# Seven places for the split weights of the upper output projection, a first half of norm 2 without GpSimd, and six FFN weight pieces split ahead

## The chip, the cores and the metric

The kernel runs on one core of one Trainium2 chip. A core has TensorE for matmuls (PE in the profile, with its weight loads as PEld), VectorE (DVE), ScalarE (ACT), GpSimd (POOL) and SyncE (SP), which here issues most DMA transfers between the chip's memory and the core's two on-chip memories, SBUF and PSUM. Each engine works through its own list of instructions in order; where one needs what another makes, it waits on a semaphore, and everything behind it in its list waits with it. The metric is the device time of one execution in microseconds (us). Three runs of the kernel before gave 3312.47, 3306.03 and 3312.3 us; their median is 3312.3 us.

## The reference, cut to what matters

One layer of a hybrid backbone is applied to 128 context tokens and 512 latent tokens, 640 tokens in all, with width D = 2048 and an FFN of width 5632. The mixers (a two-directional RWKV-7 scan and a chunked gMLP) give `[o_a, o_b]`. The change lies behind them:

```
x = x + g1 * (jnp.concatenate([o_a, o_b], axis=-1) @ lp['w_out'])
h = _rmsnorm(x, lp['norm2_g']) * (1.0 + sc2) + sh2
ff = (jax.nn.silu(h @ lp['w_ffn_gate']) * (h @ lp['w_ffn_up'])) @ lp['w_ffn_down']
return x + g2 * ff, s_fin
```

`_rmsnorm` divides each token by the root of the mean square over its 2048 channels. A final norm follows. Everything is computed in float32.

## The kernel before

Activations lie transposed, channels on the 128 partitions and tokens along the free axis: `x1T[kb]` is block kb of 16 channel blocks, 128 x 640. The 640 tokens are two halves of 320, `t1` (hf 0) and `t2` (hf 1).

A float32 product is made out of three matmuls of the type fp32r. Each operand is split into a rounded part `hi` and a rest `lo`, and for each 128 x 128 block of weights the sum of hi·hi, hi·lo and lo·hi is kept. A weight piece is 512 rows by 128 columns (256 KB), which is four blocks. `split` loads it with one DMA of SyncE into `raw` (L165), ScalarE casts it to `hi` (L166), and VectorE subtracts to get `lo` (L167). The tiles come from the pool `st` with three places each: three raw, three hi, three lo. For an FFN piece `load_plain` (L1382) and `parts` (L1391, L1392) do the same, and take their hi and lo from the same `st`.

**The upper half of the output projection.** The product with `w_out` runs in two steps; the change touches the second, over the rows of the mixer outputs whose hi and lo are `oh` and `ol`. `four_blocks(hf, m, q)` makes one piece and its 12 matmuls (L1447, L1448, L1449) for output block m, token half hf and quarter q. For hf 0 and then hf 1, for m from 0 to 15, two pieces are multiplied, so that there are 64 pieces and 768 matmuls; of hf 0 the first AHEAD = 6 pieces with q = 0 are done ahead of that loop. After each block `add_out` (VectorE, L1026) adds the result to `x1T[m]`, a DMA stores it (L1466), and `squares` squares it (ScalarE, L1412) and adds it up over a group of mostly four blocks (GpSimd, L1418). `stats` turns a group's sum into a matmul with a matrix of ones (TensorE, `ss`, L1428); after the last group of a half it makes the factor `rs` of the norm (L1431 VectorE, L1432 ScalarE, L1433 VectorE). Before, `stats` is called one block after the block that closed a group.

**Norm 2, half t1.** During hf 1, at each odd m, `first_half(m // 2)` normalizes two channel blocks of t1: GpSimd multiplies by `rs` (L1364), and VectorE multiplies and adds the modulation (L1365). For the first eight blocks `operand` also makes the FFN operand `xo`: a cast on ScalarE (L1354) and a subtraction on VectorE (L1355). GpSimd's list holds these multiplications among the sums of squares L1418 that TensorE's `ss` waits for.

**The start of the FFN.** The first two of the 44 FFN blocks (f 0 and 1 of the planner's order) are done plainly. `plain(e)` (L1534 to L1536) multiplies four pieces (gate and up weights, two channel ranges) with the operands; `first_blocks` calls plain(0) to plain(6) and does the rest of norm 2 between them: `second_half` (L1487 VectorE, L1489 ScalarE), `sums` (L1497 to L1502, VectorE), further `operand`s, `plain_out` (the gate's result, L1543 and L1544) and at the end `stores(0)`, which makes sums of the two results on GpSimd (L1703 to L1710) and stores them. Behind it the other 42 blocks run in pairs of seven products (`seven`, L1602 to L1604): GpSimd makes the combinations of weights (L1515). Their weights are loaded by `load_w` (L1688) into the pool `gu`, which has RAWB = 13 places for raw pieces and opens when the pools of the projection are closed. The loads are pulled one by one from an iterator as pieces are consumed.

A scheduler of the language sets the final place of an instruction in each engine's list, so that the order of the code is not always the order of the list.

## Time and profile before

| | us |
|---|---|
| median of three runs | 3312.3 |
| lowest and highest run | 3306.03, 3312.47 |
| profiled execution | 3317.92 |
| its span in the profile | 3316.1 |
| TensorE busy | 3151.8 (95% of the span) |
| VectorE busy | 2409.3 (73%) |
| ScalarE busy | 1452.3 (44%) |
| GpSimd busy | 1278.7 (39%) |

The profile shows one execution. Its span is the time between the first and the last recorded instruction; the execution's own time is 1.8 us more, and 5.6 us above the median of the runs. The mean clock granted to TensorE was 0.98 of full speed. TensorE is busy almost all the time; a microsecond in which it waits in the middle of the kernel, or in which its clock is lowered, is a microsecond of the kernel's time unless a later wait would have taken it anyway. The projection's second step and the start of the FFN lie from about 1462 to 1675 us of the span.

### The profile page before, as it was taken

Reading aid. Unit: us, or ns where it says so; the run is one execution under the profiler, and the core shown is the slowest. Engines: PE = TensorE matmul, PEld = TensorE weight load, DVE = VectorE, ACT = ScalarE, POOL = GpSimd, SP = SyncE. Lnnn points to the kernel's source line nnn. Section 1 sums busy time; section 2 is a strip of 40 time slices with the busy share of each in tenths; the row PEclk is TensorE's granted clock in tenths of the full one; section 3 lists DMA queues with packets and bytes.
Section 4 is the critical chain, followed back from the end, with each engine's and each line's share of the span. In section 5 each row is a group of like instructions: output and inputs, shape, how many; then the busy total and the mean of one; then the engine's idle time right before and its main releaser. Section 6 shows DMA issues by size and latency. Waiting matters only on the chain.

```text
span 3316.1 us, 72388 instructions
## 1 busy us (share of the span) xinstructions
PE 3151.8 (95%) x28216; PEld 2912.2 (88%) x28216; DVE 2409.3 (73%) x4152; ACT 1452.3 (44%) x3163; POOL 1278.7 (39%) x1114
## 2 busy tenths in 40 slices
PE   6899999999999999998999999999999999999996
PEld 3688788778877888888999999999999999999996
DVE  4448767766866677767877777877778787877787
ACT  3334444444443444334644444444444445444365
POOL 0001122222212113333155655656656555555543
PEclk8899999999999999999999999999999999999998
DMA  8767676767667488735534343443443454553453
GB/s 318 247 180 212 184 203 186 184 182 202 187 179 217 129 273 272 237 118 158 166 103 123 118 121 118 120 128 108 125 127 103 129 185 150 162 156 116 139 162 118
DMA packets 740142, 550.88 MB, mean 166 GB/s; under 512 B 140712, under 2 KB 673208, under 8 KB 730968
## 3 DMA queue, kind: packets, MB, share of 16 engines
q1 hardware_dynamic: 727480, 532.57, 53.7%
q0 software_dynamic: 9984, 13.13, 1.7%
q8 instruction: 222, 3.64, 0.5%
q14 instruction: 120, 0.98, 0.1%
q10 hardware_dynamic: 2336, 0.57, 0.1%
HBM read 437.79 MB, written 110.95 MB: 165 GB/s over the span
## 4 chain that ended last, share of the span: by engine, by line
PE 74%; DVE 10%; DMA 6%; issue 5%; POOL 3%; ACT 2%; SPq 0%; DVEq 0%; ACTq 0%; POOLq 0%
PE P L1604 15%; PE P L1603 15%; PE P L1602 15%; PE big L188 4%; PE big L190 4%; PE big L189 4%; PE pG L636 2%; PE pm L881 2%; DMA raw<-in_w_in_dram 2%; DMA wt<-in_w_mod_dram 1%; PE big L1013 1%; DVE lo L1392 1%; PE big L1449 1%; PE big L1447 1%; PE big L1448 1%
## 5 line engine op out<-in xcount | busy, mean ns | idle before, releaser
L1602 PE MATMUL P<-xo,hi 128*128 128x320 f32 x2352 | 728.2, 310 | 3.3 <-ACT hi L1391 3.3
L1604 PE MATMUL P<-xo,lo 128*128 128x320 f32 x2352 | 728.3, 310 | 2.0 <-DVE lo L1392 1.9
L1603 PE MATMUL P<-xo,hi 128*128 128x320 f32 x2352 | 728.1, 310 | 0.0
L1392 DVE TENSOR_TENSOR lo<-raw,hi 128x512 fp32r<-128x512 f32 x532 | 513.7, 969 | 169.1 <-ACT hi L1391 164.5
L1391 ACT CAST hi<-raw 128x512 fp32r<-128x512 f32 x532 | 330.7, 622 | 496.8 <-PE P L1603 389.7
L188 PE MATMUL big<-h_hi,hi 128*128 128x320 f32 x1376 | 452.3, 329 | 8.4 <-ACT hi L166 4.9
L1602 PEld LDWEIGHTS P<-xo,hi 128*128 128x128 f32 x2352 | 442.7, 188 | 3.5 <-ACT hi L1391 3.5
L1604 PEld LDWEIGHTS P<-xo,lo 128*128 128x128 f32 x2352 | 442.6, 188 | 2.8 <-DVE lo L1392 2.8
L1603 PEld LDWEIGHTS P<-xo,hi 128*128 128x128 f32 x2352 | 442.6, 188 | 0.0
L190 PE MATMUL big<-h_hi,lo 128*128 128x320 f32 x1376 | 435.1, 317 | 1.3 <-DVE lo L167 1.3
L189 PE MATMUL big<-h_lo,hi 128*128 128x320 f32 x1376 | 435.0, 316 | 0.7 <-DVE h_lo L345 0.7
L1515 POOL TENSOR_TENSOR raw<-raw 128x512 f32<-128x512 f32 x252 | 407.7, 1627 | 14.9 <-DVE lo L1392 3.3
L1604 PE MATMUL P<-xd,lo 128*128 128x320 f32 x1232 | 383.5, 311 | 14.0 <-DVE lo L1392 13.9
L1602 PE MATMUL P<-xd,hi 128*128 128x320 f32 x1232 | 382.0, 310 | 2.7 <-ACT hi L1391 0.9
L1603 PE MATMUL P<-xd,hi 128*128 128x320 f32 x1232 | 380.6, 309 | 0.0
L167 DVE TENSOR_TENSOR lo<-raw,hi 128x512 fp32r<-128x512 f32 x268 | 187.2, 701 | 218.9 <-ACT hi L166 214.8
L188 PEld LDWEIGHTS big<-h_hi,hi 128*128 128x128 f32 x1376 | 263.7, 192 | 75.7 <-issue 48.3
L166 ACT CAST hi<-raw 128x512 fp32r<-128x512 f32 x268 | 165.9, 619 | 274.7 <-PE big L189 124.4
L1391 ACT CAST hi<-rawd 128x512 fp32r<-128x512 f32 (+1 forms) x288 | 168.9, 587 | 241.5 <-PE P L1603 196.3
L189 PEld LDWEIGHTS big<-h_lo,hi 128*128 128x128 f32 x1376 | 264.3, 192 | 7.0 <-issue 3.5
L190 PEld LDWEIGHTS big<-h_hi,lo 128*128 128x128 f32 x1376 | 263.7, 192 | 7.5 <-DVE lo L167 3.0
L1604 PEld LDWEIGHTS P<-xd,lo 128*128 128x128 f32 x1232 | 231.2, 188 | 20.4 <-DVE lo L1392 19.9
(378 smaller groups left out, 6270.0 us busy)
## 6 DMA issues: line engine op xcount, KB each, us to landing
wt<-in_w_mod_dram SPq DMA_DIRECT2D x96, 1024.0 KB
raw<-in_w_ffn_gate_dram SPq DMA_DIRECT2D x182, 256.0 KB
raw<-in_w_ffn_up_dram SPq DMA_DIRECT2D x182, 256.0 KB
rec<-d_S SPq DMA_DIRECT2D x80, 576.0 KB
raw<-in_w_in_dram SPq DMA_DIRECT2D x172, 256.0 KB
rawd<-in_w_ffn_down_dram SPq DMA_DIRECT2D x128, 256.0 KB
raw<-in_w_out_dram SPq DMA_DIRECT2D x96, 256.0 KB
xd<-d_os SPq DMA_DIRECT2D x66, 320.0 KB
```

The source lines that it names most:

```text
L166: S.copy(hi, raw)
L167: V.tensor_sub(lo, raw, hi.bitcast(F32))
L188: TE.matmul(halves[hf], hi[:, k, :], h_hi[:, kb, s], start=(kb == 0), stop=False)
L189: TE.matmul(halves[hf], hi[:, k, :], h_lo[:, kb, s], start=False, stop=False)
L190: TE.matmul(halves[hf], lo[:, k, :], h_hi[:, kb, s], start=False, stop=(kb == KB - 1))
L636: TE.matmul(two[h][:, cc - c0, :], XZ[:, cc, h, :, :].rearrange("p s t -> p (s t)"), R[:, cc, :, :].rearrange("p s t -> p (s t)"), start=T ...
L1391: S.copy(hi[:, 0:nk], raw[:, 0:nk])
L1392: V.tensor_sub(lo[:, 0:nk], raw[:, 0:nk], hi[:, 0:nk].bitcast(F32))
L1515: G.tensor_tensor(out=o[:, 0:nk], in0=p[:, 0:nk], in1=q[:, 0:nk], op=ALU.subtract)
L1602: TE.matmul(ps, hi[:, k, :], xk[:, 0, :], start=f, stop=False)
L1603: TE.matmul(ps, hi[:, k, :], xk[:, 1, :], start=False, stop=False)
L1604: TE.matmul(ps, lo[:, k, :], xk[:, 0, :], start=False, stop=l)
```

## The change

Five things are changed.

1. All upper `w_out` pieces but the first six take their raw tile from a pool `wraw` with four places and hi and lo from a pool `wo` with seven places, in place of three and three.
2. `first_half` handles one channel block: VectorE multiplies by `rs`, and ScalarE applies scale and bias of the modulation in one activation. GpSimd has no part in it. It runs at m = 2 to 13 with one block each and at m = 14 and 15 with two each; the eight operand pairs are made at m = 4 to 11.
3. `stats` runs later: the oldest group is taken when m % 4 is 1, or when the group ends at block 12 or beyond.
4. Six FFN pieces are loaded into a pool `wfirst` of their own at m = 6, 7 and 8 of hf 1, and split into hi and lo tiles of the pool `pre` when the loop is over. Two more are loaded at m = 15 into `st` and split as before. These eight pieces are the whole of plain(0) and plain(1).
5. plain(0) and plain(1) run before the projection's pools are closed and without pulling loads; only then does `gu` open and do the first loads into it begin. `stores(0)` moves from the end of `first_blocks` to a hook of the first block of the seven-product stage (f = 2, third product).

```diff
-    def split(src, nk):
+    def split(src, nk, praw=None, pool=None):
         n = 512 // nk
-        raw = st.tile([P, nk, n], F32, tag="raw", name="raw", bufs=3)
-        hi = st.tile([P, nk, n], F32R, tag="hi", name="hi")
-        lo = st.tile([P, nk, n], F32R, tag="lo", name="lo")
+        praw, pool = praw or st, pool or st
+        raw, hi, lo = (p.tile([P, nk, n], t, tag=k, name=k) for p, t, k in
+                       ((praw, F32, "raw"), (pool, F32R, "hi"), (pool, F32R, "lo")))
...
-    def first_half(j):
-        for kb in (j, j + 8):
-            x = x1T[kb]
-            G.tensor_tensor(out=x[:, t1], in0=x[:, t1], in1=rs[:, t1], op=ALU.mult)
-            V.tensor_scalar(x[:, t1], x[:, t1], modc[4][:, kb, 0:1], modc[3][:, kb, 0:1], op0=ALU.mult, op1=ALU.add)
-        if j < 4:
-            operand(1, j, x1T[j][:, t1])
-            operand(2, j, x1T[j + 8][:, t1])
+    HALVES = [j + 8 * i for j in range(8) for i in range(2)]
+    def first_half(kb):
+        x = x1T[kb][:, t1]
+        V.tensor_tensor(out=x, in0=x, in1=rs[:, t1], op=ALU.mult)
+        S.activation(x, x, AF.Identity, scale=modc[4][:, kb, 0:1], bias=modc[3][:, kb, 0:1])
...
+    NPRE = 6
...
+                if i < NPRE:
+                    raw = wfirst.tile([P, 4, P], F32, tag="raw", name="raw")
+                    nc.sync.dma_start(raw, src)
+                    held_w.append(raw)
...
+    np_, wraw, pre, wo, wfirst = (phn.enter_context(tc.tile_pool(name=n, bufs=b)) for n, b in
+                          (("np", 2), ("wraw", 4), ("pre", 1), ("wo", 7), ("wfirst", NPRE)))
...
-            hf, m, sq = sqs.pop()
+            hf, m, sq = sqs.pop(0)
...
-            hi, lo = split(w_out[0, 4 * q * P:(4 * q + 4) * P, m * P:(m + 1) * P], 4)
+            hi, lo = split(w_out[0, 4 * q * P:(4 * q + 4) * P, m * P:(m + 1) * P], 4,
+                           *((wraw, wo) if q or hf or m >= AHEAD else ()))
...
-                if hf and m == KB - 1:
-                    for _ in range(3):
+                if hf and m in (6, 7, 8, KB - 1):
+                    for _ in range(2):
                         next(first)
-                if sqs:
+                if sqs and (sqs[0][1] >= 12 or m % 4 == 1):
                     stats()
...
-                if hf and m % 2:
-                    first_half(m // 2)
+                if hf and m > 1:
+                    for kb in HALVES[m - 2:m - 1] if m < 14 else HALVES[2 * m - 16:2 * m - 14]:
+                        first_half(kb)
+                    if 4 <= m < 12:
+                        j, i = divmod(m - 4, 2)
+                        operand(1 + i, j, x1T[j + 8 * i][:, t1])
+        for i, raw in enumerate(held_w):
+            hi, lo = (pre.tile([P, 4, P], F32R, tag=f"{t}{i}", name=t) for t in ("hi", "lo"))
+            S.copy(hi, raw)
+            V.tensor_sub(lo, raw, hi.bitcast(F32))
+            READY.append((hi, lo))
...
     def first_blocks():
-        plain(0)
-        plain(1)
...
-        stores(0)
...
+    loads = iter(())
+    plain(0)
+    plain(1)
+    phn.close()
+    cbx.close()
+    gux = ExitStack()
+    gu = gux.enter_context(tc.tile_pool(name="gu", bufs=2))
...
     loads = itertools.chain(first, load_w(2), load_w(3))
...
+            if f == 2 and o == 2:
+                stores(0)
```

Three places show how the lists of the engines change. In the rows that follow, a name's number tells one tile of a name from another. The first place is GpSimd's list where hf 1 of the projection begins. `sumq` are sums of squares, `sq2` a block's squares, `x1T` a block of the residual stream, and `rs2` the norm's factor. Before:

```order
L1418 TENSOR_TENSOR sumq_19345<-sumq_19302,sq2_19343 128x320
L1418 TENSOR_TENSOR sumq_19388<-sumq_19345,sq2_19386 128x320
L1364 TENSOR_TENSOR x1T_13554<-x1T_13554,rs2_18691 128x320
L1364 TENSOR_TENSOR x1T_13546<-x1T_13546,rs2_18691 128x320
L1364 TENSOR_TENSOR x1T_13553<-x1T_13553,rs2_18691 128x320
L1364 TENSOR_TENSOR x1T_13545<-x1T_13545,rs2_18691 128x320
L1364 TENSOR_TENSOR x1T_13552<-x1T_13552,rs2_18691 128x320
L1364 TENSOR_TENSOR x1T_13544<-x1T_13544,rs2_18691 128x320
L1418 TENSOR_TENSOR sumq_19478<-sq2_19434,sq2_19476 128x320
L1364 TENSOR_TENSOR x1T_13551<-x1T_13551,rs2_18691 128x320
```

After:

```order
L1425 TENSOR_TENSOR sumq_19357<-sumq_19314,sq2_19355 128x320
L1425 TENSOR_TENSOR sumq_19400<-sumq_19357,sq2_19398 128x320
L1425 TENSOR_TENSOR sumq_19490<-sq2_19446,sq2_19488 128x320
L1425 TENSOR_TENSOR sumq_19534<-sumq_19490,sq2_19532 128x320
L1425 TENSOR_TENSOR sumq_19580<-sumq_19534,sq2_19578 128x320
L1425 TENSOR_TENSOR sumq_19674<-sq2_19624,sq2_19672 128x320
L1425 TENSOR_TENSOR sumq_19727<-sumq_19674,sq2_19725 128x320
```

The sixteen multiplications by the factor are gone from this list, and one sum of squares follows the other.

The second place is SyncE's list where the projection ends and the FFN's weights begin. `d_x1` is the store of a block, and `raw` from `in_w_ffn_*` is an FFN piece. The last two pieces into `st` and, before, the first into `gu` (from the row with `raw_20184` on) stand there. Before:

```order
L165 DMA raw_20119<-in_w_out_dram 128x4x128
L1382 DMA raw_20137<-in_w_ffn_gate_dram 128x4x128
L1466 DMA d_x1_93<-x1T_13541 128x320
L1382 DMA raw_20139<-in_w_ffn_gate_dram 128x4x128
L1382 DMA raw_20141<-in_w_ffn_up_dram 128x4x128
L1466 DMA d_x1_93<-x1T_13540 128x320
L1466 DMA d_x1_93<-x1T_13539 128x320
L1382 DMA raw_20184<-in_w_ffn_up_dram 128x4x128
L1382 DMA raw_20186<-in_w_ffn_gate_dram 128x4x128
L1382 DMA raw_20188<-in_w_ffn_gate_dram 128x4x128
```

After (`in_w_out` is the last piece of the projection):

```order
L165 DMA raw_20143<-in_w_out_dram 128x4x128
L1474 DMA d_x1_93<-x1T_13544 128x320
L1474 DMA d_x1_93<-x1T_13543 128x320
L1474 DMA d_x1_93<-x1T_13542 128x320
L1474 DMA d_x1_93<-x1T_13541 128x320
L1474 DMA d_x1_93<-x1T_13540 128x320
L1474 DMA d_x1_93<-x1T_13539 128x320
L1387 DMA raw_20334<-in_w_ffn_gate_dram 128x4x128
L1387 DMA raw_20336<-in_w_ffn_gate_dram 128x4x128
L1387 DMA raw_20338<-in_w_ffn_up_dram 128x4x128
```

After, all loads of pieces for plain(0) and plain(1) stand further up in the list, the last stores of the projection follow each other, and the row with `raw_20334`, the first into `gu`, belongs to plain(2), where before it belonged to plain(0).

The third place is VectorE's list at the end of plain(6), where the first block of seven products begins. `lo` from `raw` is the rest of a weight piece (the first two in each fence are the first two of that block, L1392 before and L1397 after), `xo` an operand, `act` a plain block's result. Before:

```order
L1355 TENSOR_TENSOR xo_21011<-x1T_13553,xo_21011 128x320
L1355 TENSOR_TENSOR xo_21014<-x1T_13552,xo_21014 128x320
L1355 TENSOR_TENSOR xo_21017<-x1T_13551,xo_21017 128x320
L1355 TENSOR_TENSOR xo_20947<-x1T_13552,xo_20947 128x320
L1355 TENSOR_TENSOR xo_20956<-s3_20954,xo_20956 128x320
L1544 TENSOR_TENSOR act_20689<-pa_20999,C_20565 128x320
L1355 TENSOR_TENSOR xo_20975<-x1T_13550,xo_20975 128x320
L1355 TENSOR_TENSOR xo_20979<-x1T_13542,xo_20979 128x320
L1392 TENSOR_TENSOR lo_21040<-raw_20698,hi_21039 128x512
L1355 TENSOR_TENSOR xo_20984<-s3_20982,xo_20984 128x320
L1355 TENSOR_TENSOR xo_20989<-x1T_13549,xo_20989 128x320
L1392 TENSOR_TENSOR lo_21045<-raw_20717,hi_21044 128x512
```

After:

```order
L1554 TENSOR_TENSOR act_20694<-pa_21006,C_20747 128x320
L1355 TENSOR_TENSOR xo_21033<-x1T_13549,xo_21033 128x320
L1355 TENSOR_TENSOR xo_21018<-x1T_13554,xo_21018 128x320
L1397 TENSOR_TENSOR lo_21043<-raw_20764,hi_21042 128x512
L1355 TENSOR_TENSOR xo_20957<-x1T_13552,xo_20957 128x320
L1355 TENSOR_TENSOR xo_21021<-x1T_13553,xo_21021 128x320
L1355 TENSOR_TENSOR xo_21024<-x1T_13552,xo_21024 128x320
L1355 TENSOR_TENSOR xo_21027<-x1T_13551,xo_21027 128x320
L1554 TENSOR_TENSOR act_20699<-pa_21009,C_20575 128x320
L1355 TENSOR_TENSOR xo_20966<-s3_20964,xo_20966 128x320
L1355 TENSOR_TENSOR xo_20985<-x1T_13550,xo_20985 128x320
L1355 TENSOR_TENSOR xo_20989<-x1T_13542,xo_20989 128x320
```

The first rest of a weight piece (`lo_21040` before, `lo_21043` after) has moved up past an `act` and several operands.

More of the change, by code (lines that the diff above doesn't have):

```diff
@@ L1393, in parts @@
         return hi, lo
+    phn = ExitStack()
+    np_, wraw, pre, wo, wfirst = (phn.enter_context(tc.tile_pool(name=n, bufs=b)) for n, b in
+                          (("np", 2), ("wraw", 4), ("pre", 1), ("wo", 7), ("wfirst", NPRE)))
     with ExitStack() as ph:
-        np_ = ph.enter_context(tc.tile_pool(name="np", bufs=2))
         pss = ph.enter_context(tc.tile_pool(name="pss", bufs=1, space=PSUM))
@@ L1473, in flow_step @@
     obx.close()
-    cbx.close()
-    gux = ExitStack()
-    gu = gux.enter_context(tc.tile_pool(name="gu", bufs=2))
-    gus.append(gu)
-    xcp = xcx.enter_context(tc.tile_pool(name="xcp", bufs=1, side="right"))
-    xdp = xdx.enter_context(tc.tile_pool(name="xdp", bufs=1, side="right"))
     def second_half(j):
@@ L1690, in load_w @@
                     yield
+    loads = iter(())
[5 more added lines that the diff above has]
+    gu = gux.enter_context(tc.tile_pool(name="gu", bufs=2))
+    gus.append(gu)
+    xcp = xcx.enter_context(tc.tile_pool(name="xcp", bufs=1, side="right"))
+    xdp = xdx.enter_context(tc.tile_pool(name="xdp", bufs=1, side="right"))
     loads = itertools.chain(first, load_w(2), load_w(3))
```

14 lines of the change are left out of this document (8 added, 6 removed).

## The prediction

> **What bounds the kernel now.** I read the page's head first:
>
> ```profile
> span 3316.1 us, 72388 instructions
> PE 3151.8 (95%) x28216; PEld 2912.2 (88%) x28216; DVE 2409.3 (73%) x4152; ACT 1452.3 (44%) x3163; POOL 1278.7 (39%) x1114
> ```
>
> TensorE is the bound of the whole, so the question is only where it stands still or runs at a lowered clock around the change. The table of stretches shows that, in the order: span of the stretch, its length, then busy time and instructions of PE, PEld, DVE, ACT and POOL, granted clock, DMA share, GB/s. The first two rows are the projection's two halves, the third its end, the fourth and fifth places in the FFN's start, the last the FFN behind them.
>
> ```profile
> 1462.50:1524.00 61.50, 59.50 (x399) 58.50 (x398) 34.72 (x56) 30.12 (x53) 9.73 (x11) 1.00 0.62 187
> 1524.00:1596.00 72.00, 62.21 (x391) 59.72 (x389) 55.66 (x97) 34.72 (x66) 29.54 (x27) 0.95 0.50 150
> 1595.70:1598.70 3.00, 1.62 (x6) 0.60 (x5) 1.77 (x4) 1.32 (x3) 0.00 (x0) 1.00 0.16 55
> 1612.50:1619.50 7.00, 4.94 (x22) 4.41 (x21) 6.49 (x15) 5.68 (x14) 0.00 (x0) 0.76 0.73 206
> 1657.70:1675.00 17.30, 10.45 (x46) 9.79 (x47) 13.96 (x22) 7.24 (x17) 7.64 (x7) 0.70 0.25 74
> 1675.00:1900.00 225.00, 225.00 (x1536) 225.00 (x1535) 172.47 (x217) 97.50 (x170) 133.67 (x91) 1.00 0.40 120
> ```
>
> The last row has TensorE busy for all of its 225 us: what is won or lost ahead of 1675 is passed on to the end undiminished. It also gives the undisturbed pace, 225.00 / 1536 = 0.1465 us a matmul. Where the idle time sits, the timeline of PE tells; the bracket is the idle time before a row, and what ended it.
>
> ```profile
> 1468.73 0.41 PE L1449 MATMUL big<-oh,lo 128*128 128x320 f32 x1 [0.45 <-DVE lo L167]
> 1484.33 0.81 PE L1428 MATMUL ss<-sumq,ones 128*128 128x320 f32 x2 [1.55 <-POOL sumq L1418]
> 1536.08 0.41 PE L1449 MATMUL big<-oh,lo 128*128 128x320 f32 x1 [2.98 <-DVE lo L167]
> 1539.50 0.63 PE L1449 MATMUL big<-oh,lo 128*128 128x320 f32 x1 [1.27 <-DVE lo L167]
> 1548.26 0.41 PE L1449 MATMUL big<-oh,lo 128*128 128x320 f32 x1 [1.20 <-DVE lo L167]
> 1552.43 0.81 PE L1428 MATMUL ss<-sumq,ones 128*128 128x320 f32 x2 [2.44 <-POOL sumq L1418]
> 1569.21 0.81 PE L1428 MATMUL ss<-sumq,ones 128*128 128x320 f32 x2 [1.90 <-POOL sumq L1418]
> 1597.06 0.81 PE L1428 MATMUL ss<-sq,ones 128*128 128x320 f32 x2 [0.79 <-ACT sq L1412]
> 1598.45 0.41 PE L1534 MATMUL C<-xo,hi 128*128 128x320 f32 x1 [0.58 <-DVE rs L1431]
> 1614.09 0.42 PE L1534 MATMUL C<-xo,hi 128*128 128x320 f32 x1 [1.30 <-ACT hi L1391]
> 1615.42 0.44 PE L1536 MATMUL C<-xo,lo 128*128 128x320 f32 x1 [0.77 <-DVE lo L1392]
> 1659.42 0.41 PE L1536 MATMUL C<-xo,lo 128*128 128x320 f32 x1 [1.73 <-DVE lo L1392]
> 1664.71 0.64 PE L1602 MATMUL P<-xo,hi 128*128 128x320 f32 x1 [3.27 <-ACT hi L1391]
> 1667.47 0.64 PE L1604 MATMUL P<-xo,lo 128*128 128x320 f32 x1 [1.86 <-DVE lo L1392]
> ```
>
> The first seven lie in the projection: 0.45 + 1.55 + 2.98 + 1.27 + 1.20 + 2.44 + 1.90 = 11.8 us, four times for a weight's lo, three times for a sum of squares. Why lo is late, the groups of instructions tell: the first row is a stretch of hf 0 (1488 to 1524), the others are the start of hf 1 (1532 to 1552).
>
> ```profile
> L167 DVE TENSOR_TENSOR lo<-raw,hi 128x512 fp32r<-128x512 f32 x21 | 14.5, 692 | 11.9 <-ACT hi L166 11.9
> ...
> L167 DVE TENSOR_TENSOR lo<-raw,hi 128x512 fp32r<-128x512 f32 x7 | 8.7, 1264 | 0.0
> L1026 DVE SCALAR_TENSOR_TENSOR x1T<-big,modc,x1T 128x192 f32<-128x192 f32 (+1 forms) x6 | 1.9, 355 | 0.0
> L1364 POOL TENSOR_TENSOR x1T<-x1T,rs 128x320 f32<-128x320 f32 x16 | 17.2, 1110 | 6.6 <-DVE rs L1433 6.6
> L1418 POOL TENSOR_TENSOR sumq<-sumq,sq 128x320 f32<-128x320 f32 x2 | 2.1, 1060 | 0.1
> ```
>
> While GpSimd does its sixteen multiplications of 1110 ns nearly back to back, a lo costs VectorE 1264 ns in place of 692 and VectorE never idles; and a sum of squares that stands behind those multiplications on GpSimd keeps TensorE's `ss`, and so everything behind it, waiting.
>
> **The change part by part.**
>
> *Projection.* Idle 11.8 us, and a clock of 0.95 over the 72 us of hf 1, which is 0.05 x 72 = 3.6 us of lost pace: 15.4 us to be had. Counted the other way: of the 399 + 391 instructions about 772 are blocks, 113.1 us at the pace above, and nine `ss` pairs at some 0.6 us of own time each are 5.4; 133.5 less 118.5 is 15.0. Two of the three edits meet the same waits. Without the sixteen L1364 rows GpSimd has only sums left, and VectorE should be back at 692 ns. Seven places let hi and lo run five pieces ahead, 5 x 12 x 0.1465 = 8.8 us, more than the longest wait of 2.98. The later `stats` gives a sum up to two more pieces, 3.5 us, more than its longest wait of 2.44. I take all but 0.5 us, for the first waits at 1468, where the pieces ahead still come from three places: +14.9 (bounds 11 and 15.4).
>
> Does VectorE have room in hf 1 for what it takes over? Further prices are from rows of the FFN's start:
>
> ```profile
> 1602.22 1.29 DVE L1487 TENSOR_TENSOR x1T<-x1T,rs 128x320 f32<-128x320 f32 x3
> 1602.74 0.93 ACT L1489 ACTIVATE x1T<-x1T,modc,modc 128x192 f32<-128x192 f32 x2
> 1662.90 0.48 DVE L1355 TENSOR_TENSOR xo<-x1T,xo 128x320 fp32r<-128x320 f32 x1
> 1596.54 0.47 ACT L1412 ACTIVATE sq<-x1T 128x320 f32<-128x320 f32 x1 [0.26 <-DVE x1T L1026]
> 1600.90 0.62 ACT L1391 CAST hi<-raw 128x512 fp32r<-128x512 f32 x1 [2.00 <-DMA raw<-in_w_ffn_up_dram]
> ```
>
> VectorE: 32 lo at 0.69 are 22.1, 32 parts of `add_out` at 0.355 are 11.4, 16 multiplications at 1.29 / 3 = 0.43 are 6.9, 8 xo at 0.48 are 3.8, eight FFN lo 5.5: 49.7 us of the 384 x 0.1465 + 6 x 0.6 = 60 us that TensorE needs for hf 1. The 16 L1365 it had are gone to ScalarE, whose list comes to 32 + 8 casts at 0.62, 16 squares at 0.47, 16 activations at up to 0.6 and 8 xo at about 0.47, 45.7 us. Both fit, and a lead of several pieces takes up the unevenness of their order. On SyncE's queue six loads of 256 KB now go out among the projection's. At 0.87 us each (worked out below) they add 5.2 us of transfer; the DMA share is 0.62 and 0.50 in the projection's two rows, and four raw places in flight cover the delay of a neighbour. I take nothing for them; the cover is gone if a piece comes later than the lead of 8.8 us.
>
> *End of the projection.* Three xo casts of some 0.47 us now stand ahead of the last square on ScalarE, and they wait for the projection's last matmul; 0.26 us of idle and `add_out` lie beside them. I take 1.0 us (0.4 to 1.4). TensorE's idle time there grows from 0.79 + 0.58 = 1.4 to about 2.4 us. Does that cost clock? In the row 1612.5 to 1619.5 it stands still for only 1.30 + 0.77 us, and the clock is 0.76, that is 0.24 x 7 = 1.7 us; at 1552 it stood for 2.44 us. Weighted at four in ten: 0.7 us. The Trainium skill ("TensorE: Matmul & The Clock Gate", Part 1: The HAM clock gate) says that the clock is halved after an idle window of about 3.4 us, and that the windows run freely. By it no pause quoted here would halve the clock, and the sum would be 0.7 us better; the row with 0.76 after 2.07 us speaks against it.
>
> *plain(0) and plain(1).* 96 matmuls, 14.1 us, with all weights split: TensorE waits for nothing. Meanwhile, though, no FFN piece is loaded into `gu`: the first load waits until the third of the four accumulators is done, 10.6 us into plain(0). What it takes from there is in two rows, a first load issued and its cast (the row at 1600.90 above):
>
> ```profile
> 1597.90 0.38 SPq L1382 DMA_DIRECT2D raw<-in_w_ffn_up_dram  x1
> DMA packets 6055, 3.02 MB, mean 302 GB/s; under 512 B 184, under 2 KB 6053, under 8 KB 6053
> ```
>
> Issue to cast is 1600.90 - 1597.90 = 3.0 us. So hi is ready at 10.6 + 3.0 + 0.6 = 14.2 and lo, behind xo on VectorE, at about 15.7, while TensorE wants them at 14.1: it waits some 1.5 us, and pays clock with a chance of six in ten (1.0). Later pieces land at 256 KB / 302 GB/s = 0.87 us each, and TensorE eats one in 12 x 0.1465 = 1.76. Before, this place lost 7.0 - 22 x 0.1465 = 3.8 us. I take +1.0 (bounds -10, by the late loads of the rival below, and +3.8).
>
> *End of plain(6).* Before, 17.3 - 46 x 0.1465 = 10.6 us are lost. VectorE is what is late: among its rows there, beside GpSimd's sums of `stores(0)`, are
>
> ```profile
> 1663.86 0.87 POOL L1703 TENSOR_TENSOR s<-act 128x320 f32<-128x320 f32 x1 [5.04 <-DVE xo L1355]
> 1664.10 2.04 DVE L1355 TENSOR_TENSOR xo<-x1T,xo 128x320 fp32r<-128x320 f32 x2
> 1666.07 1.35 DVE L1392 TENSOR_TENSOR lo<-raw,hi 128x512 fp32r<-128x512 f32 x1
> ```
>
> so that a lo takes 1.35 us there. In the new list the first lo of the seven products stands ahead of an `act` and several xo, and four fewer stand ahead of the second: 4 x 0.48 = 1.9 us of VectorE, twice that when slowed. `stores(0)` has moved in the code but stands in the same place among GpSimd's rows, right behind the first four combinations, so its slowing stays. I take +4 (bounds -3, as the xo come later by what they let pass, and +8).
>
> *Sum.* 14.9 - 1.0 - 0.7 + 1.0 + 4.0 = 18.2 us. The profiled execution's 3317.9 would become 3299.7. That execution is 5.6 us above the median of the runs; the saving lies in one place and should be the same in both, so the median goes from 3312.3 to 3294.1.
>
> **The rivals.** About 0.2%, 6.6 us, is what a measurement of this kernel tells from no change.
>
> *Only the projection gains.* The waits at 1614 and 1659 to 1675 are the work of VectorE's long list at the FFN's start, and a TensorE that arrives earlier may only find it later there. For it: the list is as long as before, but for what was split ahead. Then the sum is 14.9 - 1.7 = 13.2, 3299; with 4 us lost again, 3303.
>
> *VectorE becomes the bound in hf 1.* If each sum on GpSimd (12 in hf 1, 1.06 us) holds VectorE up for its whole length, 49.7 + 12.7 = 62.4 us exceed TensorE's 60 and half of the waits stay: 3312.3 - 7.7 + 1.7, or 3306, and to 3312 if the xo and activations, chained from VectorE to ScalarE and back, queue in front of the casts. Against it: the row of 692 ns, in a stretch that has such sums too. The Trainium skill ("SBUF — State Buffer", SBUF: two separate sides) says that a GpSimd instruction and one of VectorE with two SBUF inputs exclude each other for the whole instruction; the 692 ns beside GpSimd's sums show little of it, the 1264 ns much.
>
> *The late opening of `gu` makes it slower.* The first load may be released only by the last matmul of plain(1), at 14.1, and thirteen loads issued at once may share the queues rather than come one by one: 13 x 0.87 = 11.3 us for the first. Then TensorE waits 3.0 + 11.3 + 1.3 = 15.6 us at plain(2), and half as much again goes to the clock (at 1659 to 1675, 6.9 us of waits cost 10.6). That is 23.4, less the 3.8 paid before, against 13.2 won: 6.4 us slower, 3319. It decides from a wait of 11.3 us on (1.5 x 11.3 = 17). Against it: at 1597 to 1601 a first load, with others issued behind it, was usable after 3.0 us.
>
> **How the numbers follow.** My forecast 0.55, only the projection 0.18, VectorE bound 0.12, `gu` late 0.15. Faster takes the first two and a quarter of the third, 0.76; within 0.2% is most of the rest of the third and a little of the fourth, 0.10; slower the rest, 0.14. The forecast's own range goes from the upper bounds of its terms, 15.4 - 0.4 + 3.8 + 8 = 26.8 and so 3285.5, to 3303; 3283 leaves room for a median that falls as low as the lowest of three runs may (3306.03 before). To hold eight in ten I go up to 3312, which takes in the first rival whole and the second for the most part.
>
> **What the profile will show.** Right: no wait for lo or a sum from 1470 to the projection's end, which comes 133.5 - 14.9 = 118.6 us after 1462.5, give or take 2; lo near 692 ns in hf 1; TensorE without a break in plain(0) and plain(1); a wait of 1 to 3 us at plain(2); less than 7 us lost where the seven products begin. Wrong: VectorE's lo still over 1 us in hf 1; a wait above 5 us at plain(2); waits grown behind plain(6), which would take back what the projection gave.

## The result, and the profile after

The changed kernel took 3288.47 us in the median of four runs (3284.2 to 3292.71), the kernel before 3312.39 us beside it: a ratio of 0.9937, with a 95% interval of 0.9925 to 0.9950. The prediction was 3294.1 with a range of 3283 to 3312. In a second comparison (below) the medians were 3290.24 and 3308.37 us, 18.1 us apart, a ratio of 0.9943 (0.9930 to 0.9956).

The page's head for the changed kernel; its execution took 3287.43 us:

```profile
span 3285.6 us, 72386 instructions
PE 3141.3 (96%) x28216; PEld 2905.3 (88%) x28216; DVE 2401.2 (73%) x4152; ACT 1458.3 (44%) x3179; POOL 1260.1 (38%) x1098
```

The span is 30.5 us shorter than that of before. That is more than the medians show, and where it comes from is seen best by cutting both spans at the same instructions. The starts of the projection's upper half are in these rows of the lo matmuls (number of them, shortest, median and longest duration, start of the first and of the last): before, after, and the kernel before in a second profile.

```profile
L1449 PE MATMUL big<-oh,lo x256: 308/309/633, 1462.8 to 1595.4; 128*128 128x320 f32 x128
```

```profile
L1457 PE MATMUL big<-oh,lo x256: 304/308/468, 1448.8 to 1569.4; 128*128 128x320 f32 x128
```

```profile
L1449 PE MATMUL big<-oh,lo x256: 307/309/570, 1451.3 to 1584.3; 128*128 128x320 f32 x128
```

The changed kernel came to the projection 14.0 us earlier, but the second profile of the kernel before, with nothing changed, did so 11.5 us earlier than the first. All engines' lists are the same in both kernels up to there, but for one load that SyncE issues 1.1 us ahead of that point (1447.42 below). So these 14 us are taken as scatter between executions, and only what follows as the change's. All stretches, in us, each from the first start of one group to the next (the last start of the projection's lo matmuls ends the first stretch):

| | before | before, again | after | after, again |
|---|---|---|---|---|
| projection's upper half | 132.9 | 133.3 | 120.9 | 122.1 |
| to the first plain block | 3.1 | 3.0 | 3.4 | 3.4 |
| plain blocks, to the first of seven products | 62.5 | 61.0 | 60.2 | 60.6 |
| seven products, to the last on the first operands | 1043.8 | 1043.4 | 1040.6 | 1040.5 |
| the rest | 611.3 | 611.3 | 612.0 | 612.2 |
| sum | 1853.6 | 1852.0 | 1837.1 | 1838.8 |

In this sum the first pair saved 16.5 us and the second 13.2. The timeline of TensorE after the change has these waits from 1448 to 1645 us; they answer to the fourteen of before that the prediction lists.

```profile
1472.02 1.11 PE L1435 MATMUL ss<-sumq,ones 128*128 128x320 f32 x2 [2.23 <-POOL sumq L1425]
1571.36 0.81 PE L1435 MATMUL ss<-sq,ones 128*128 128x320 f32 x2 [1.15 <-ACT sq L1419]
1572.75 0.41 PE L1544 MATMUL C<-xo,hi 128*128 128x320 f32 x1 [0.58 <-DVE rs L1438]
1587.61 0.42 PE L1544 MATMUL C<-xo,hi 128*128 128x320 f32 x1 [0.51 <-ACT hi L1396]
1589.10 0.42 PE L1546 MATMUL C<-xo,lo 128*128 128x320 f32 x1 [0.93 <-DVE lo L1397]
1628.92 0.41 PE L1546 MATMUL C<-xo,lo 128*128 128x320 f32 x1 [0.84 <-DVE lo L1397]
1631.42 0.41 PE L1546 MATMUL C<-xo,lo 128*128 128x320 f32 x1 [0.48 <-DVE lo L1397]
1633.63 0.41 PE L1611 MATMUL P<-xo,lo 128*128 128x320 f32 x1 [0.19 <-DVE lo L1397]
1636.36 0.41 PE L1609 MATMUL P<-xo,hi 128*128 128x320 f32 x1 [0.71 <-ACT hi L1396]
1638.80 0.41 PE L1611 MATMUL P<-xo,lo 128*128 128x320 f32 x1 [1.88 <-DVE lo L1397]
```

Of the projection's 11.8 us of waits 2.2 are left, one wait for a sum at its start (3.02 us in the second profile). The stretches (columns as before: PE, PEld, DVE, ACT, POOL, clock, DMA share, GB/s) show what the clock did:

```profile
1448.50:1510.00 61.50, 59.27 (x389) 58.41 (x388) 41.29 (x66) 35.21 (x63) 9.78 (x11) 0.97 0.84 241
1510.00:1570.50 60.50, 60.21 (x401) 58.89 (x399) 41.94 (x87) 36.81 (x71) 14.21 (x11) 1.00 0.49 147
1585.00:1592.00 7.00, 5.56 (x37) 5.03 (x36) 5.96 (x14) 5.68 (x14) 0.00 (x0) 1.00 1.01 293
1626.00:1645.00 19.00, 14.90 (x83) 13.19 (x82) 17.38 (x26) 9.43 (x21) 10.40 (x9) 0.91 0.32 99
1645.00:1870.00 225.00, 225.00 (x1536) 225.00 (x1535) 170.72 (x217) 97.45 (x170) 137.01 (x92) 1.00 0.40 120
```

The second half, which took 72 us with a clock of 0.95, now runs at 1.00 without a wait. The first half has become the worse one: a clock of 0.97 over 61.5 us, and a DMA share of 0.84 in place of 0.62.

### The profile page after: what moved, and what is told of

It reads as the page before. It is cut to its first block, busy times and chain, and to the rows that moved or that the text cites. A ratio compares the mean times of both kernels' runs of the same rounds, so it can differ in the third digit from the quotient of the medians.

```text
span 3285.6 us, 72386 instructions
## 1 busy us (share of the span) xinstructions
PE 3141.3 (96%) x28216; PEld 2905.3 (88%) x28216; DVE 2401.2 (73%) x4152; ACT 1458.3 (44%) x3179; POOL 1260.1 (38%) x1098
## 4 chain that ended last, share of the span: by engine, by line
PE 75%; DVE 9%; issue 6%; DMA 5%; POOL 3%; ACT 2%; SPq 0%; DVEq 0%; ACTq 0%; POOLq 0%
PE P L1611 15%; PE P L1609 15%; PE P L1610 15%; PE big L188 4%; PE big L190 4%; PE big L189 4%; PE pG L636 2%; PE pm L881 2%; DMA raw<-in_w_in_dram 2%; PE big L1455 1%; PE big L1456 1%; PE big L1457 1%; DMA wt<-in_w_mod_dram 1%; PE pblk L820 1%; DVE mx L781 1%
## 5 line engine op out<-in xcount | busy, mean ns | idle before, releaser
L1397 DVE TENSOR_TENSOR lo<-raw,hi 128x512 fp32r<-128x512 f32 x526 | 507.3, 967 | 171.4 <-ACT hi L1396 167.3
L167 DVE TENSOR_TENSOR lo<-raw,hi 128x512 fp32r<-128x512 f32 x268 | 185.1, 693 | 204.7 <-ACT hi L166 198.3
```

Of the source, the lines that this page charges most:

```text
L167: V.tensor_sub(lo, raw, hi.bitcast(F32))
L1397: V.tensor_sub(lo[:, 0:nk], raw[:, 0:nk], hi[:, 0:nk].bitcast(F32))
```

## The experiments

Times are medians, each beside runs of the kernel before on the same chip; the stretches are from one profile of each kernel, cut as in the table above. Two profiles of one kernel differ by 0.4 us (before) and 1.2 us (after) in the projection, so that is what a single profile can tell there.

**The kernel before, again.** Nothing is changed.

> The kernel before once more, for its profile alone. The changed kernel's profile reaches the first matmul of the projection's upper half at 1448.5 us, the one of before at 1462.6, though all engines have the same lists up to there. If these 14.0 us are scatter from one execution to the next, this profile has that point anywhere from 1448 to 1463 and the span from there to the end again near 1853.6 us (within 2). If the change itself speeds up what lies ahead of it, this profile has the point at 1462 or later.

Its row stands above: the projection starts at 1451 us, and 1852.0 us follow. The expectation for scatter holds; the early start of the changed kernel's profile is scatter. The 68 runs of the kernel before that stand beside the experiments agree with it: they lie between 3299.55 and 3316.97 us.

**Seven places alone.**

```diff
-            hi, lo = split(w_out[...], 4)
+            hi, lo = split(w_out[...], 4, *((wraw, wo) if q or hf or m >= AHEAD else ()))
```

> The kernel before with four raw and seven hi and lo places for the projection's upper half, and nothing else. Theory (lead cures the late lo, GpSimd's list the late sums): the four waits for lo go, 5.9 us, and with them some of the 3.6 us of clock; the three waits for a sum, 5.9 us, stay. Projection from 132.9 to 125 to 128 us, the whole 5 to 8 us faster. Rival (VectorE at 1264 ns a lo is the bound of that stretch, and a lead only delays the wait): the lo waits shrink by less than 2 us, the whole is 0 to 2 us faster.

3308.69 against 3307.84 us, ratio 1.0003 (0.9992 to 1.0014): nothing, and my theory falls. The projection took 133.8 us. The time is the rival's, though its sign is not: one wait for a lo, of 2.42 us, is left, so these waits shrank by 3.5 us and not by less than 2. TensorE's waits in hf 1, and GpSimd's list beside them:

```profile
1534.29 0.61 PE L1451 MATMUL big<-oh,lo 128*128 128x320 f32 x1 [2.42 <-DVE lo L167]
1544.07 1.43 PE L1429 MATMUL ss<-sumq,ones 128*128 128x320 f32 x2 [6.77 <-POOL sumq L1419]
```

```profile
1529.35 1.12 POOL L1419 TENSOR_TENSOR sumq<-sq,sq 128x320 f32<-128x320 f32 x1
1530.44 10.18 POOL L1364 TENSOR_TENSOR x1T<-x1T,rs 128x320 f32<-128x320 f32 x9
1540.58 1.11 POOL L1419 TENSOR_TENSOR sumq<-sumq,sq 128x320 f32<-128x320 f32 x1
1541.65 1.10 POOL L1364 TENSOR_TENSOR x1T<-x1T,rs 128x320 f32<-128x320 f32 x1
1542.71 1.30 POOL L1419 TENSOR_TENSOR sumq<-sumq,sq 128x320 f32<-128x320 f32 x1
```

Nine multiplications stand in GpSimd's list between one sum and the next, and the group's sum is ready at 1544.0. The sum's matmul so begins 91.2 us after the projection's start (1452.9), where before it began 89.9 us after it (1552.43 and 1462.5): the lead does not bring it forward. With a lead for lo, TensorE comes to it sooner and waits 6.77 us there in place of 2.44.

**The first half of norm 2 alone.**

```diff
-            G.tensor_tensor(out=x[:, t1], in0=x[:, t1], in1=rs[:, t1], op=ALU.mult)
-            V.tensor_scalar(x[:, t1], ...)
+        V.tensor_tensor(out=x, in0=x, in1=rs[:, t1], op=ALU.mult)
+        S.activation(x, x, AF.Identity, ...)
```

> The kernel before with the first half of norm 2 on VectorE and ScalarE in place of GpSimd and VectorE, and nothing else. Theory (GpSimd's sixteen multiplications are the cause of both kinds of waits in hf 1): 2.98 + 1.27 + 1.20 + 2.44 + 1.90 us of waits and 3.6 us of clock go, projection from 132.9 to 119 to 123 us, 10 to 14 us faster. Rival (VectorE, which takes the multiplications over with three places for lo, is the bound in hf 1): lo waits stay or grow, projection above 127 us, less than 6 us faster.

3303.36 us, ratio 0.9977 (0.9964 to 0.9990). The projection fell to 125.0 us, 7.9 less, which lies between theory and rival; the whole, 4.5 us faster, is in the rival's range. Of waits above 0.2 us there were left in the projection:

```profile
1474.18 0.81 PE L1426 MATMUL ss<-sumq,ones 128*128 128x320 f32 x2 [1.52 <-POOL sumq L1416]
1545.42 0.42 PE L1447 MATMUL big<-oh,lo 128*128 128x320 f32 x1 [0.40 <-DVE lo L167]
1549.94 0.54 PE L1426 MATMUL ss<-sumq,ones 128*128 128x320 f32 x1 [2.78 <-POOL sumq L1416]
```

At the start of hf 1 (1522 to 1542) VectorE's and GpSimd's groups are:

```profile
L167 DVE TENSOR_TENSOR lo<-raw,hi 128x512 fp32r<-128x512 f32 x11 | 8.1, 753 | 0.9 <-ACT hi L166 0.9
L1365 DVE TENSOR_TENSOR x1T<-x1T,rs 128x320 f32<-128x320 f32 x10 | 4.7, 480 | 0.0
L1416 POOL TENSOR_TENSOR sumq<-sumq,sq 128x320 f32<-128x320 f32 x2 | 2.7, 1357 | 3.7 <-issue 2.7 <-ACT sq L1410 1.0
```

The mechanism is the theory's: a lo takes 753 ns where it took 1264 beside GpSimd's multiplications, and the waits for a lo in hf 1 fell from 5.45 us to 0.40. The rival's sign, waits for a lo that stay or grow, is not there.

**Split ahead alone** (with plain(0) and plain(1) ahead of the pool, and the later `stores(0)`; `split`, `first_half` and `stats` as before).

> The kernel before with the six pieces split ahead, plain(0) and plain(1) ahead of the opening of the FFN's pool, and the sums of the first two blocks' results moved, and nothing of the projection's places, norm 2 or sums changed. Theory (the gain at the FFN's start is its own): from the projection's last matmul to the end of the first chunk of seven products 3 to 6 us less, projection within 3 us of 132.9, the whole 2 to 7 us faster. Rival (the early loads and splits load the DMA queues and VectorE in the projection, where lo is late already): projection 3 us or more longer, the whole within 3 us of before.

3307.29 us, ratio 0.9998 (0.9987 to 1.0008). Projection 134.1, plain blocks 61.1, seven products 1038.7: against the second profile of before, 4.6 us less in the FFN's start and 0.8 more in the projection. The profile bears out the theory for these stretches; the whole, 0.6 us faster, lies outside the theory's 2 to 7 us and inside the rival's 3. From the projection on it took 1849.9 us, 2.1 less than that profile of before.

**First half and later sums**, without places and without pieces split ahead.

```diff
-            hf, m, sq = sqs.pop()
+            hf, m, sq = sqs.pop(0)
...
-                if sqs:
+                if sqs and (sqs[0][1] >= 12 or m % 4 == 1):
```

> The kernel before with the first half of norm 2 off GpSimd and the sums' matmuls later, with three places as before and nothing split ahead. With only the first half moved the projection took 125.0 us, and waits for a sum of 1.52 and 2.78 us and a lo of 0.57 us in all were left. Theory (places aren't needed, a later sum's matmul takes the rest): projection 120 to 122 us, the whole 10 to 13 us faster. Rival (seven places are what the later sums need, since with three a wait only moves on to a lo): projection 123 to 126 us, the whole no more than 9 us faster.

3290.59 us beside 3308.37, ratio 0.9948 (0.9936 to 0.9961). That is 17.8 us faster, and the projection took 119.0 us, both better than the theory had it. One wait of TensorE is left in the projection:

```profile
1460.12 0.41 PE L1447 MATMUL big<-oh,lo 128*128 128x320 f32 x1 [0.31 <-DVE lo L167]
```

The later sum's matmul takes 6.0 us more off the projection than the first half alone, and with three places no lo in hf 1 is late enough to show. These two parts give as much as the whole change, to within what the medians tell: 3290.59 us here and 3290.24 for the changed kernel on the same chip. From the projection's start to the last product on the first operands this profile takes 1225.9 us, and the two of the changed kernel 1225.1 and 1226.6.

**All but the pieces split ahead.**

> The changed kernel without the six pieces split ahead: places, first half and later sums as changed, the FFN's start as before. Theory (the 2.23 us wait for a sum and the lowered clock at the start of the changed kernel's projection come from the FFN pieces that are loaded early): projection 117.5 to 120 us, below the 120.9 of the changed kernel; from there to the first chunk's end as before, 1108 to 1110 us; the whole 11 to 16 us faster. Rival (the wait is the places' own, as the run with places alone has 2.03 us of it too): projection 120 to 122 us.

3298.3 us, ratio 0.9967 (0.9953 to 0.9980): 10.1 us faster, less than the theory's 11 to 16. The projection took 117.6 us, so the wait of 2.23 us and the lower clock of the changed kernel do come with the pieces split ahead, as the theory had it (0.26 us of it is left). But from there to the end of the first chunk it took 1112.3 us, over the 1108 to 1110 expected. The plain blocks took 66.8 us in place of 61.0 in the second profile of before, and these waits stand in and behind them:

```profile
1587.97 0.63 PE L1538 MATMUL C<-xo,hi 128*128 128x320 f32 x1 [2.47 <-ACT hi L1389]
1640.59 0.41 PE L1606 MATMUL P<-xo,hi 128*128 128x320 f32 x1 [3.71 <-ACT hi L1389]
```

The run with places alone has the same two waits, 2.47 and 3.71 us, and 64.8 us in its plain blocks; the runs with three places and nothing split ahead have 1.3 to 1.5 and 3.3. It is not that the first load into the late pool comes later: SyncE issues it 0.55 us ahead of plain(0) here (1569.08) as before (1597.90). The larger part of the 5.8 us is clock, 0.92 over the 66.8 us here where it was 1.00 over those 61.0. What sets the longer waits off was not tried. As far as these two profiles show, the places cost here, and the pieces split ahead make up for it.

**The changed kernel, again.**

> The changed kernel once more, for more executions of it and of before on one chip. From the projection's start to the end its profile saved 16.5 us, while the medians of four runs each are 23.9 apart. Theory (what lies ahead of the projection is the same in both and only scatters): 14 to 19 us faster here, and the profile's start of the projection anywhere in 1446 to 1464 us. Rival (the change saves time ahead of it too): 22 us or more faster, start of the projection below 1450 us.

18.1 us faster, projection from 1452.2 us: the theory holds, in the upper part of its range. The wait for the first sum is there again, at 3.02 us, with a clock of 0.97 over the first 61.5 us.

**The early loads held in place.**

```diff
-                    nc.sync.dma_start(raw, src)
+                    tc.keep_in_program_order(nc.sync.dma_start(raw, src))
                     held_w.append(raw)
```

> The changed kernel with the six FFN loads held at their place in the code (m = 6 to 8 of the second half) in place of where the scheduler put them, among the first loads of the first half. Theory (these loads delay the projection's own pieces, and so VectorE's list and the first sum): the wait of 2.23 us for a sum at 1472 falls below 1.6 us, DMA share of the projection's first 61.5 us from 0.84 to 0.7 or less, the whole 1 to 3 us faster than the changed kernel. Rival (the wait is due to blocks that are finished twice as fast at the start, and the loads don't matter): wait and time as in the changed kernel within 1 us.

In the changed kernel the scheduler had put the six loads, written at m = 6 to 8 of hf 1, among the first loads of hf 0. Three rows of SyncE in the changed kernel, with four of them:

```profile
1447.42 0.37 SPq L1382 DMA_DIRECT2D raw<-in_w_ffn_gate_dram  x1
1454.25 2.12 SPq L1382 DMA_DIRECT2D raw<-in_w_ffn_up_dram  x2
1471.64 0.69 SPq L1382 DMA_DIRECT2D raw<-in_w_ffn_gate_dram  x1
```

Held in place, they are issued from 1524 to 1534. The projection then takes 117.5 us, 3.4 and 4.6 less than in the two profiles of the changed kernel, and the first stretch's row reads:

```profile
1454.20:1515.70 61.50, 61.37 (x412) 60.36 (x411) 39.28 (x63) 34.31 (x60) 10.71 (x12) 1.00 0.76 225
```

No wait for a sum is left in it, though two pieces into `st` still go out early (1459.95). The DMA share fell to 0.76, not to 0.7. The median, 3290.94 us, is that of the changed kernel beside it (3290.24); in this one profile the rest of the kernel took 615.9 us in place of 612, with a granted clock of 0.97 in one stretch of 100 us there. That the early loads made the wait is shown; by which path, late pieces of the projection or VectorE's list, was not separated. That the kernel got faster by holding them is not shown by this run alone: the 1 to 3 us of the theory are not in the medians.

**Loads held, sums one block later, GpSimd's four instructions later.**

```diff
-                total = np_.tile([P, HALF], F32, tag="sumq", name="sumq")
+                total = np_.tile([P, HALF], F32, tag="sumq", name="sumq", bufs=3)
...
-                if sqs and (sqs[0][1] >= 12 or m % 4 == 1):
+                if sqs and (sqs[0][1] >= 12 or m % 4 == (1 if hf else 2)):
...
-        G.tensor_tensor(out=s3, in0=a11, in1=a21, op=ALU.subtract)
+        ins = G.tensor_tensor(out=s3, in0=a11, in1=a21, op=ALU.subtract)
+        if p == 0:
+            tc.keep_in_program_order(ins)
...
-            if f == 2 and o == 2:
+            if f == 2 and o == 4:
```

> The changed kernel with the six FFN loads held at their place in the code, the sums of the first half's groups one block later, and the four GpSimd instructions on the first two blocks' results held behind the weight combinations of the next block. Theory (VectorE is slowed at the start of the seven products by those four, 1.35 us a lo): the wait of 1.9 us at the last lo there goes, the stretch from the first product to the first chunk's end falls from 1040.5 to 1037.5 to 1039, from the projection's start to the end 1834 to 1836 us; 20 to 24 us faster than before. Rival (the operands ahead of that lo on VectorE are what is late): stretch 1040 to 1041, 17 to 20 us faster.

3294.03 us, ratio 0.9948 (0.9934 to 0.9963): 15.0 us faster, less than theory and rival had it, though the profile's 1835.3 us from the projection's start to the end are in the theory's range. The stretch of the seven products fell to 1037.8 us as the theory had it, but the plain blocks rose to 64.4. The list of ScalarE had changed with the edit: sixteen operand casts stand ahead of the first hi.

```profile
1585.86 5.87 ACT L1354 CAST xo<-x1T 128x320 fp32r<-128x320 f32 x16
1591.62 1.66 ACT L1396 CAST hi<-raw 128x512 fp32r<-128x512 f32 x3
```

TensorE waited 2.96 us for that hi. One gain was given back by another engine's order.

**Loads held, places as before** (three).

> The changed kernel with the six FFN loads held at their place in the code, and the projection's places as before (three). Theory (the places do nothing once GpSimd is clear and the sums come later): projection 117.5 to 119.5 us, the whole within 2 us of the same kernel with the places (3290.9). Rival (the splits ahead load VectorE and ScalarE, and only the lead of seven places hides that): waits for lo in the second half, projection over 120 us.

3294.66 us beside 3309.01, ratio 0.9955 (0.9941 to 0.9969); projection 122.0 us. Small waits came back in hf 1 (0.17, 0.33, 0.38 and 0.17 us, for lo and once for hi); they are 1.05 us of the 4.5 that the projection is longer than with the places (117.5). TensorE's weight loads (PEld) waited 3.2 us for lo and 0.8 us for hi between 1516 and 1576, and their waits don't all show as idle time of the matmuls. The projection over 120 us and the late lo are the rival's signs, and the theory's 117.5 to 119.5 us is missed: with the extra splits the lead of seven places is worth some 4 us of the projection, in one profile each, without them about 1.4 (119.0 against 117.6 above), which two profiles hardly tell from scatter. The medians of two kernels from different chips, 3.7 us apart, don't tell more.

**The multiplications back on GpSimd.**

```diff
-        V.tensor_tensor(out=x, in0=x, in1=rs[:, t1], op=ALU.mult)
+        G.tensor_tensor(out=x, in0=x, in1=rs[:, t1], op=ALU.mult)
```

> The changed kernel with the sixteen multiplications by the norm's factor back on GpSimd (the scale and bias stay on ScalarE, all else as changed). Theory (these multiplications are the cause that the other parts can't make up for): lo at about 1.2 us again at the start of hf 1, waits for a sum or a lo of 5 us or more together, projection 127 us or more, no more than 12 us faster than before. Rival (lead of the places and the later sums suffice to hide them): projection 120 to 123 us as in the changed kernel, 16 us or more faster.

3305.67 us, ratio 0.9983 (0.9969 to 0.9996): most of the gain is gone by this one line. The theory's times for the waits, the projection and the whole hold. The projection took 132.7 us, and its loss in hf 1 is one wait and the clock behind it (0.93 over the 40.2 us from 1544 on):

```profile
1544.42 1.43 PE L1435 MATMUL ss<-sumq,ones 128*128 128x320 f32 x2 [9.23 <-POOL sumq L1425]
```

A lo took VectorE 931 ns over 1518 to 1575. With seven places TensorE did not wait for it; the sum that stands behind the multiplications it did wait for, later `stats` or not.

**Loads and GpSimd's four instructions held, sums as changed.**

> The changed kernel with the six FFN loads held at their place in the code and the four GpSimd instructions on the first two blocks' results held behind the next block's weight combinations; the sums as in the changed kernel, and ScalarE's order at the FFN's start as there. Theory (the two gains are each their own): projection 117.5, plain blocks 60.4, seven products to the first chunk's end 1037.8, together with the 3.4 between 1219 us, where the changed kernel's two profiles have 1225.1 and 1226.6; 23 to 25 us faster than before. Rival (the sixteen VectorE operands there are late in any case, and what is not lost to GpSimd is lost to them): 1222 us or more, 17 to 20 us faster.

3284.87 us (3281.58 to 3295.45) beside 3306.32, ratio 0.9941 (0.9925 to 0.9957). Projection 117.5, to the plain blocks 3.4, plain blocks 60.0, seven products 1038.5: 1219.4 us, as the theory had it, where the changed kernel has 1225.1 and 1226.6. What moved at the seven products is VectorE's last late lo, 0.69 us in place of 1.35, TensorE's wait for it, 0.53 in place of 1.88, and the clock, 1.00 in place of 0.91:

```profile
1638.04 0.41 PE L1611 MATMUL P<-xo,lo 128*128 128x320 f32 x1 [0.53 <-DVE lo L1397]
1626.00:1645.00 19.00, 16.23 (x103) 14.91 (x102) 17.34 (x29) 10.29 (x23) 8.39 (x6) 1.00 0.30 86
```

It is the fastest median of all, 21.5 us below the kernel before, which lies between the theory's 23 to 25 and the rival's 17 to 20. Its interval overlaps that of the changed kernel; that it is the faster of the two is seen in the stretches of its one profile, 5.7 to 7.2 us, and not by the ratios.

## Why the prediction was right

The sum of the prediction was 18.2 us, and its main mechanism holds: the waits of hf 1 come from GpSimd's list, and go when it is cleared. From the projection's start on, the two pairs of profiles saved 16.5 and 13.2, the medians 23.9 and 18.1. By its steps:

- *Projection, predicted 14.9.* Measured 12.0 (132.9 to 120.9). The waits in hf 1 and their clock went wholly, as said. What failed is "I take nothing for them", the step on the six loads: it had them among the projection's loads, but not at its start, where the scheduler put them, and where they cost 3.4 us (117.5 when held). Two of its signs fell by this: a wait for a sum came behind 1470 (2.23 us at 1472), and the projection was shorter by 12.0 us where 14.9, give or take 2, was to be seen. The step that sets the seven places' lead of 8.8 us against the longest wait for a lo credits them with something that they don't give: places alone won nothing, since hf 1 hung on GpSimd's list. The first half and the later sums do it, 7.9 and 6.0 us.
- *VectorE's room in hf 1, 49.7 of 60 us.* It was enough; the busy time of VectorE in the second stretch is 41.9 of 60.5, with 27 of the 32 lo and none of the eight FFN lo in it. A multiplication cost 568 ns there (8.9 us for 16) where the row of 430 was used, and a lo 730 for 692. The second rival, VectorE as the bound, is out. (It counts 12 sums in hf 1; GpSimd's 27 instructions in the row of before, less 16 multiplications, are 11.)
- *End of the projection, predicted -1.0 and -0.7 of clock.* Measured -0.3 (3.1 to 3.4): the three casts were mostly hidden. TensorE stood still for 1.15 + 0.58 = 1.7 us, and the clock stayed at 1.00. In plain(0) and plain(1) it then ran without a break, as said: 96 matmuls in 14.05 us.
- *plain(0) to plain(2), predicted a wait of 1.5 us.* Measured 0.51 + 0.93 = 1.44. The first load into the late pool was issued 10.9 us after plain(0) began (predicted 10.6), and its hi began 3.3 us later (predicted 3.0):

```profile
1583.67 0.93 SPq L1387 DMA_DIRECT2D raw<-in_w_ffn_gate_dram  x2
1586.94 0.62 ACT L1396 CAST hi<-raw 128x512 fp32r<-128x512 f32 x1 [0.96 <-DMA raw<-in_w_ffn_gate_dram]
```

  With the clock at 1.00 the place lost 7.0 - 37 x 0.1465 = 1.6 us in place of 3.8: 2.2 won, predicted 1.0. The third rival, a late first piece that makes it slower, is out: 1.44 us in place of 15.6.
- *End of plain(6), predicted +4.* It lost 19.0 - 83 x 0.1465 = 6.8 us in place of 10.6: 3.8. That `stores(0)` would go on slowing VectorE was right; holding it back gave another 2.1 us (1040.6 to 1038.5).

So the prediction named the right places, and that its sum came out near the measured one is in part luck: the projection's term was too high by 3 us and the two terms behind it, the end of the projection and the wait at plain(2), too low by 2.6 together. What the pieces split ahead win at the FFN's start beside the run with the first half and the later sums alone, 2.3 to 2.6 us in the plain blocks and the seven products, they cost at the projection's start, 1.9 to 3.1 us, so that those two parts are as fast as the whole change. The remaining difference between 18.2 and 23.9 us is not explained by any stretch behind the projection's start; with 18.1 in the second comparison, scatter is the likely reason. That was not settled further.

On the clock, the two readings stayed apart: by the Trainium skill ("TensorE: Matmul & The Clock Gate", Part 1: The HAM clock gate) an idle window of about 3.4 us is needed to halve it. After 1.7 us of waits at the projection's end the clock was 1.00, in accord with that; after one wait of 2.23 us at 1472 it was lowered, which is not. The 0.97 over 61.5 us is some 4 us at a little over half the clock, right behind that wait. In the first three rows, of the changed kernel, it is 0.60, 0.55 and 1.00; the last row is the kernel before, behind its wait of 2.44 us.

```profile
1472.00:1474.00 2.00, 1.98 (x7) 1.71 (x8) 1.67 (x3) 1.26 (x3) 0.32 (x1) 0.60 0.94 280
1474.00:1476.00 2.00, 2.00 (x10) 2.00 (x10) 0.00 (x0) 0.00 (x0) 0.55 (x1) 0.55 0.98 272
1476.00:1478.00 2.00, 2.00 (x16) 2.00 (x15) 0.61 (x2) 1.26 (x3) 0.00 (x0) 1.00 1.13 347
1552.00:1554.00 2.00, 1.57 (x9) 1.41 (x10) 2.00 (x6) 0.47 (x1) 0.38 (x1) 1.00 0.43 128
```

So the length of a wait does not decide alone in these traces: 2.23 us lowered the clock and 2.44 us did not. The same pair of waits at the projection's end left it at 1.00 in the changed kernel, and in the run without the pieces split ahead (1.16 + 0.58 us) it was 0.62 and 0.53 from 1570 to 1574. What decides was not found.

## What to carry to other kernels

When an engine waits for two kinds of things, look whether both hang on one list of a third engine: with more places for the one, TensorE here only reached the other sooner, and waited there. Take the long work out of the list that the short, awaited work stands in, or let it be asked for later. A load that waits for nothing can be put by the scheduler far ahead of its place in the code, and cost there; look where it stands in the queue. And try the parts of a change alone: here two of five gave all of the gain.

## What was not expected of the hardware

- Two executions of one kernel differed by 11.5 us in the first 1450 us, with the same lists. Rows of the same work show it growing: the modulation's matmuls, in the first and the second profile of the kernel before, begin within 0.3 us of each other, and the last of them begins at 1097.8 and 1087.7 us.

```profile
L881 PE MATMUL pm<-wt,cT x512: 591/592/1057, 149.0 to 1097.8; 128*2 128x512 f32 x171
```

```profile
L881 PE MATMUL pm<-wt,cT x512: 591/592/1061, 149.3 to 1087.7; 128*2 128x512 f32 x171
```

- GpSimd's sums of squares are slower in hf 1 too. They take 882 to 892 ns on average in hf 0 of both kernels; in hf 1 the first sums of a group took 963 ns before and 1584 after, the others 1225 and 1125. That VectorE's instructions beside them do it, as GpSimd's do to a lo, is likely but was not tried.

```profile
L1418 POOL TENSOR_TENSOR sumq<-sumq,sq 128x320 f32<-128x320 f32 x7 | 8.6, 1225 | 14.0 <-ACT sq L1412 8.2 <-issue 5.8
L1418 POOL TENSOR_TENSOR sumq<-sq,sq 128x320 f32<-128x320 f32 x4 | 3.9, 963 | 18.4 <-ACT sq L1412 18.4
L1425 POOL TENSOR_TENSOR sumq<-sumq,sq 128x320 f32<-128x320 f32 x7 | 7.9, 1125 | 17.6 <-ACT sq L1419 12.3 <-issue 4.4 <-POOL sumq L1425 0.9
L1425 POOL TENSOR_TENSOR sumq<-sq,sq 128x320 f32<-128x320 f32 x4 | 6.3, 1584 | 22.8 <-ACT sq L1419 22.8
```
